# Conditioning projections of a two-layer diffusion trunk: from three ways of computing a block to one multiply-and-sum over transposed weights

## The chip, the cores and the metric

The kernel runs on one core of a Trainium2 chip. The metric is the device time of one execution in microseconds, as a median over runs. Engines are named as in the profile: PE (TensorE), DVE (VectorE), ACT (ScalarE), POOL (GpSimd) and SP (SyncE, which asks for most transfers). One core has 16 DMA engines.

## The reference, cut to what matters

Two layers over 512 latent tokens (128 to a tile) of width 1024, beside 256 context tokens that live through layer 0 only. Each layer begins with the six vectors of its adaptive norm:

```python
def ada_params(cond, w, b):          # cond (1, 1024), w (1024, 6144), b (6144)
    return jnp.split(jax.nn.silu(cond) @ w + b, 6, axis=-1)

for l in range(2):
    sh1, sc1, g1, sh2, sc2, g2 = ada_params(c, w_ada[l], b_ada[l])
    a = rms_norm(h, g_norm1[l]) * (1 + sc1) + sh1
    y = attention_mixer(a, ...) if l == 0 else conformer_conv(a, ...)
    h = h + g1 * y
    h = h + g2 * peer_ffn(rms_norm(h, g_norm2[l]) * (1 + sc2) + sh2, ...)
```

So per layer a matrix of 1024 x 6144 (24 MB) is multiplied by one row. `peer_ffn` scores 16 sets of 128 keys for each token, takes the best 16 of each, combines them, and mixes the values of 16 experts for each of 8 heads out of 16384 experts. The attention mixer has eight global heads with low-rank projections (`cq`, `ckv`) and eight neighbourhood heads (`qn`, `kn`, `vn`).

## The kernel before

One vector of 1024 is eight **blocks** of 128 columns; a layer has 48 blocks, numbered f = 0 to 47. Shifts and scales are needed as columns (`par`, 128 partitions x 48), the gates (blocks 16 to 23 and 40 to 47) as rows spread over all partitions, kept in DRAM (`g1d`, `g2d`) until they are used. A block's weights come as one tile `ada_w`, 128 x 8 x 128 floats, 512 KB in pieces of 512 bytes. Layer 0's blocks 0 to 15, which both the latent and the context tokens need first, are summed on PE in a prologue (lines 971 to 1005); this stays. The other 80 are spread over the kernel and computed in three ways:

- **On DVE, as eight small products** (lines 766 to 768): layer 0's blocks 16 to 23, at every second step of the input projections. A step is a quarter of one product (`quarter`, two of eight slices of the inner dimension, for 4 or 6 token tiles; products ckv, cq, kn, qn, vn of widths 288, 384, 512, 512, 512 with 6, 4, 6, 4, 6 token tiles, so 20 quarters). A sum of ones on PE (line 907) and an addition on DVE (908) make it a row in all partitions, which SP stores. The weights of a quarter are split into a high part (ACT) and a remainder (DVE, `w_lo`, line 1043), the latter just ahead of its use.
- **On POOL** (lines 779 to 782): layer 0's blocks 24 to 39, in attention, one at every fourth unit of the neighbourhood heads and at every second of the global heads (a head has four units). A transposition on PE (900) and a sum and an addition on DVE (902, 903) end each.
- **On PE, sixteen products of matrix by column or column by matrix** (819, 821): 14 blocks of layer 1 between the heads of the first PEER's query stage (line 282, one each, two in the first two), 4 more in its gate stage (line 533), and 8 of layer 1's in the second PEER's query stage.
- **In the first PEER's main loop**, as eight products on DVE, four per round, and a sum of ones on PE (866 to 887): 30 blocks. The tile for them has one buffer.

A PEER stage has these parts in order. The query stage: 16 halves of heads, each a product of 24 matmuls on PE (`s`, lines 145 to 147), a score product (`scp`, 260) and top-16 searches on DVE; then seven chunks of the expert product (`EARLY`). A gate stage in which DVE builds one-hot tiles (`eij`, `ahl`, lines 456 and 458) and PE multiplies them. The main loop of 128 rounds, of which the first 96 compute a chunk ahead (three matmuls per slice, `s1`), take its activation (line 313), prepare values and gates (`prep`, 582 to 600) and add up the output (605); POOL fetches rows of experts for the last token tile (616), and DVE multiplies and sums them (624, 628).

Each engine works in its program's order. SP's requests also wait in order: a load waits until its buffer is free, and every later request of SP behind it.

Of the kernel before, what the change touches and what calls it, by code (L numbers as in the profile page):

```python
# [1 line left out]

# [37 lines left out]
B0, B1, B2, B3, FRONT_TWICE = 8, 6, 20, 40, (0, 1)  # L40

# [3 lines left out]
HOW = "vga"  # L45
ADA_KV = (3,)
ADA_NOT = tuple(range(4, 20, 2))
# [102 lines left out]
def peer(k, h, xr, h_done, A, sh, g2d, wq, sk, uT, un, vn, out_open, out_cb, side=None, front=None, slow=None):  # L150
# [116 lines left out]
    front_step = front and front(qp, lambda: psf.tile([128, TT, 128], F32, name="gp", bufs=4))  # L267
# [48 lines left out]
    while front_step is not None and front_step():  # L316
        pass
# [164 lines left out]
    side_step = side and side(gp, lambda: psf.tile([128, TT, 128], F32, name="scp", bufs=2))  # L482

# [32 lines left out]
    for b in range(nb):  # L516
# [15 lines left out]
        if side_step is not None:  # L532
            side_step()
    while side_step is not None and side_step():
        pass
# [42 lines left out]
    def prep(c, cu=None):  # L578
# [6 lines left out]
        w = bs.tile([128, NTD], F32, name="w_f", bufs=2)  # L585
# [5 lines left out]
        nc.vector.tensor_tensor(w.rearrange("p (b t) -> p b t", t=SB), ring.pop(c).rearrange("p (b t) -> p b t", t=SB),  # L591
# [79 lines left out]
    beside = slow(bs) if slow is not None else None  # L671
    if beside is not None:
        next(beside)
# [4 lines left out]
    for m in range(NCHUNK):  # L678
# [8 lines left out]
        if c < NCHUNK:  # L687
            room = s1p[c][:, NTD:T]
            s1_gelu(c)
# [58 lines left out]
class Ada:  # L748
# [3 lines left out]
    def __init__(self, k, l, cond, w, bT, brow):  # L752
        self.k, self.l, self.cond, self.w, self.bT, self.brow = k, l, cond, w, bT, brow
        self.par = k.const.tile([128, 48], F32, name="ada_par%d" % l)

    def load(self, pool, f0, bufs):
        t = pool.tile([128, KD, 128], F32, name="ada_w", bufs=bufs)
        self.k.nc.sync.dma_start(t, self.w[:, f0:f0 + 128].rearrange("(kk p) f -> p kk f", p=128))
        return t

    def partial(self, how, t, acc):

        nc = self.k.nc
        c = self.cond
        if how == "v":
            nc.vector.tensor_scalar(acc, t[:, 0, :], c[:, 0:1], None, op0=OP.mult)
            for kk in range(1, KD):
                nc.vector.scalar_tensor_tensor(acc, t[:, kk, :], c[:, kk:kk + 1], acc, op0=OP.mult, op1=OP.add)
            return
        g = nc.gpsimd  # L770
        for kk in range(KD):
            if how == "a" or (how == "m" and kk % 2):
                nc.scalar.activation(t[:, kk, :], t[:, kk, :], AF.Copy, scale=c[:, kk:kk + 1])
        if how == "m":
            t2 = t.rearrange("p (k two) f -> p k two f", two=2)[:, :, 0, :]
            g.tensor_tensor(t2, t2, c.rearrange("p (k two) -> p k two", two=2)[:, :, 0:1].to_broadcast([128, 4, 128]),
                            op=OP.mult)
        if how == "g":
            g.tensor_tensor(t, t, c[:, :, None].to_broadcast([128, KD, 128]), op=OP.mult)
        g.tensor_tensor(t[:, 0:4, :], t[:, 0:4, :], t[:, 4:8, :], op=OP.add)  # L780
        g.tensor_tensor(t[:, 0:2, :], t[:, 0:2, :], t[:, 2:4, :], op=OP.add)
        g.tensor_tensor(acc, t[:, 0, :], t[:, 1, :], op=OP.add)

    def stepper(self, pool, psum, blocks, eng, g1_dst, g2_dst, lag=1, wbufs=2):

        nc = self.k.nc
        todo, loaded, accs, stores = list(blocks), [], [], []

        def reduce(f, acc):
            p = psum()  # L790
            if f // 8 in (2, 5):
                o = f % 8 * 128
                br = pool.tile([128, 128], F32, name="ada_br", bufs=lag)
                nc.sync.dma_start(br, row_bcast(self.brow[f * 128:(f + 1) * 128], 128))
                self.bcast(p[:, 0, :], acc[:, 0, :], br, br)
                stores.append(((g1_dst if f < 24 else g2_dst)[:, o:o + 128], br))
            else:
                self.columns(p, acc, f, 1)

        summed = []  # L800

        def on_pe():

            if stores:
                nc.sync.dma_start(*stores.pop(0))
            if summed:
                f, p, br = summed.pop(0)
                if br is None:
                    nc.vector.tensor_tensor(self.par[:, f:f + 1], p[:, 0, 0:1], self.bT[:, f:f + 1], op=OP.add)
                else:  # L810
                    nc.vector.tensor_tensor(br, p[:, 0, :], br, op=OP.add)
                    o = f % 8 * 128
                    stores.append(((g1_dst if f < 24 else g2_dst)[:, o:o + 128], br))
            if loaded:
                f, t, br = loaded.pop(0)
                p, c = psum(), self.cond
                for kk in range(KD):
                    if br is None:
                        nc.tensor.matmul(p[:, 0, 0:1], lhsT=t[:, kk, :], rhs=c[:, kk:kk + 1], start=(kk == 0), stop=(kk == KD - 1))
                    else:  # L820
                        nc.tensor.matmul(p[:, 0, :], lhsT=c[:, kk:kk + 1].to_broadcast([128, 128]), rhs=t[:, kk, :],
                                         start=(kk == 0), stop=(kk == KD - 1))
                summed.append((f, p, br))
            if todo:
                f, br = todo.pop(0), None
                if f // 8 in (2, 5):
                    br = pool.tile([128, 128], F32, name="ada_br", bufs=wbufs + 2)
                    nc.sync.dma_start(br, row_bcast(self.brow[f * 128:(f + 1) * 128], 128))
                loaded.append((f, self.load(pool, f * 128, wbufs), br))
            return bool(todo or loaded or stores or summed)  # L830
        if eng == "p":
            return on_pe

        def step():
            if stores:
                nc.sync.dma_start(*stores.pop(0))
            if len(accs) == lag or accs and not loaded:
                reduce(*accs.pop(0))
            if loaded:
                f, ts = loaded.pop(0)  # L840
                acc = pool.tile([128, 1, 128], F32, name="ada_acc", bufs=lag)
                self.partial(eng, ts, acc[:, 0, :])
                accs.append((f, acc))
            if todo:
                f = todo.pop(0)
                loaded.append((f, self.load(pool, f * 128, wbufs)))
            return bool(todo or loaded or accs or stores)
        return step

    def slow(self, pool, blocks, dst=None):  # L850


        nc, c = self.k.nc, self.cond
        blocks, after = list(blocks), []

        def load(f):
            br = None
            if f // 8 in (2, 5):
                br = pool.tile([128, 128], F32, name="ada_br", bufs=2)
                nc.sync.dma_start(br, row_bcast(self.brow[f * 128:(f + 1) * 128], 128))  # L860
            return self.load(pool, f * 128, 1), br

        def products(t, acc, kks):
            for kk in kks:
                if kk == 0:
                    nc.vector.tensor_scalar(acc, t[:, kk, :], c[:, kk:kk + 1], None, op0=OP.mult)
                else:
# [1173 lines left out]
```

## Time and profile before

| | us |
|---|---|
| median of three runs | 3344.88 |
| the three runs | 3340.55, 3344.88, 5339.81 |
| the profiled execution | 3343.83 |
| its span, first to last instruction | 3342.1 |
| PE busy | 3207.8 |
| DVE busy | 2576.0 |
| ACT busy | 1288.2 |
| POOL busy | 976.1 |

The profile is one execution. Busy times are sums over an engine's instructions; an engine that waits for a semaphore isn't busy. The mean granted clock of PE is 0.982 of its full speed. In the windows the stages are: 0 to 66 us prologue, 66 to 243 input and low-rank projections, 243 to 512 attention with its output product, 512 to 670 the first PEER's query stage, 670 to 868 its gates, 868 to 1805 its main loop and end, 1805 to 2065 the convolution, 2065 to 3342 the second PEER in the same order.

### The profile page before, as it was taken

How to read it: one execution, taken by the hardware profiler on the slowest of the kernel's cores; microseconds unless marked ns; L12 is line 12 of the kernel's file. 1: busy time of each engine (PE TensorE's matmuls, PEld its weight loads, DVE VectorE, ACT ScalarE, POOL GpSimd, SP SyncE). 2: the span in 40 equal slices, each digit the busy share in tenths (PEclk: the TensorE clock that was granted, in tenths of full speed). 3: DMA queues.
4: the chain of work that ended last, by engine and by line, in shares of the span. 5: the costliest groups of instructions: out<-in, count | busy, mean ns of one | idle time of the engine just before them, and what ended most of it. 6: DMA issues, size and time to landing. Idle time of an engine off the chain costs nothing.

```text
span 3342.1 us, 45728 instructions
## 1 busy us (share of the span) xinstructions
PE 3207.8 (96%) x16982; PEld 2783.6 (83%) x16982; DVE 2576.0 (77%) x4732; ACT 1288.2 (39%) x2065; POOL 976.1 (29%) x800
## 2 busy tenths in 40 slices
PE   8889999988999999999999998988999999999999
PEld 5775568978999999999987867888999999999987
DVE  3657736889688888888876976899777777777777
ACT  3435533345433333333335234235533333333333
POOL 1347412300033333443430001320033333344330
PEclk9989999999999999999999998999999999999999
DMA  6412124346799999899893113326789888989985
GB/s 199 130 46 79 57 82 152 114 164 252 269 337 328 324 342 333 318 339 336 307 320 119 51 45 112 117 86 247 266 285 314 313 310 315 313 309 314 314 311 180
DMA packets 373679, 764.34 MB, mean 229 GB/s; under 512 B 24144, under 2 KB 221008, under 8 KB 366160
## 3 DMA queue, kind: packets, MB, share of 16 engines
q1 hardware_dynamic: 292816, 442.62, 38.8%
q0 software_dynamic: 73728, 268.47, 22.9%
q10 hardware_dynamic: 6912, 50.33, 3.7%
q8 instruction: 133, 2.18, 0.3%
q14 instruction: 90, 0.74, 0.1%
HBM read 702.61 MB, written 58.72 MB: 228 GB/s over the span
## 4 chain that ended last, share of the span: by engine, by line
PE 83%; DVE 11%; issue 3%; DMA 1%; ACT 1%; SPq 1%; POOL 0%; ACTq 0%; POOLq 0%; DVEq 0%
PE acc L605 30%; PE s L145 11%; PE s L147 11%; PE s L146 11%; DVE eij L456 3%; PE y L1636 2%; PE cz L145 2%; PE cz L147 2%; PE cz L146 2%; DVE ahl L458 1%; PE z L147 1%; PE z L145 1%; PE z L146 1%; PE ot L1421 1%; DVE u_lo L176 1%
## 5 line engine op out<-in xcount | busy, mean ns | idle before, releaser
L146 PE MATMUL s<-hhi,u_lo 128*128 128x384 f32 (+1 forms) x2304 | 791.2, 343 | 14.4 <-DVE u_lo L176 14.2
L145 PE MATMUL s<-hhi,u_hi 128*128 128x384 f32 (+1 forms) x2304 | 798.6, 347 | 3.0 <-ACT u_hi L172 3.0
L147 PE MATMUL s<-hlo,u_hi 128*128 128x384 f32 (+1 forms) x2304 | 790.6, 343 | 0.0
L616 POOL DMA_INDIRECT row<-in_u_dram,eidx x256 | 313.2, 1224 | 954.2 <-DVE row L624 455.7
L616 POOL DMA_INDIRECT row<-in_v_dram,eidx x256 | 348.8, 1362 | 518.8 <-DVE gacc L628 448.4
L582 ACT ACTIVATE v_hi<-v_raw 128x1024 fp32r<-128x1024 f32 x192 | 203.8, 1062 | 679.0 <-PE acc L605 609.9
L146 PEld LDWEIGHTS s<-hhi,u_lo 128*128 128x128 f32 x2304 | 436.2, 189 | 33.2 <-DVE u_lo L176 17.4
L584 DVE TENSOR_TENSOR v_lo<-v_raw,v_hi 128x1024 fp32r<-128x1024 f32 x192 | 235.2, 1225 | 291.4 <-ACT v_hi L582 275.8
L145 PEld LDWEIGHTS s<-hhi,u_hi 128*128 128x128 f32 x2304 | 436.4, 189 | 18.8 <-ACT u_hi L172 3.7
L147 PEld LDWEIGHTS s<-hlo,u_hi 128*128 128x128 f32 x2304 | 435.6, 189 | 10.2
L605 PE MATMUL acc<-v_hi,w_hi 128*128 128x512 f32 x1344 | 417.4, 391 | 0.8 <-ACT w_hi L593 0.8
L605 PE MATMUL acc<-v_hi,w_lo 128*128 128x512 f32 x1344 | 416.2, 391 | 0.0
L605 PE MATMUL acc<-v_lo,w_hi 128*128 128x512 f32 x1344 | 415.9, 390 | 0.0
L176 DVE TENSOR_TENSOR u_lo<-u_raw,u_hi 128x1024 fp32r<-128x1024 f32 x242 | 295.1, 1219 | 48.1 <-ACT u_hi L172 48.0
L628 DVE SCALAR_TENSOR_TENSOR gacc<-row,gwgt,gacc 128x1024 f32<-128x1024 f32 x254 | 325.6, 1282 | 4.7
L172 ACT ACTIVATE u_hi<-u_raw 128x1024 fp32r<-128x1024 f32 x288 | 302.3, 1050 | 14.6 <-ACT stg L475 11.0
L624 DVE SCALAR_TENSOR_TENSOR row<-row,hg 128x1024 f32<-128x1024 f32 x256 | 300.6, 1219 | 0.0
L605 PEld LDWEIGHTS acc<-v_lo,w_hi 128*128 128x128 f32 x1344 | 252.3, 188 | 55.9
L605 PEld LDWEIGHTS acc<-v_hi,w_lo 128*128 128x128 f32 x1344 | 252.2, 188 | 54.6
L605 PEld LDWEIGHTS acc<-v_hi,w_hi 128*128 128x128 f32 x1344 | 249.5, 188 | 40.8 <-ACT w_hi L593 1.2
L593 ACT ACTIVATE w_hi<-w_f 128x384 fp32r<-128x384 f32 x256 | 134.7, 526 | 319.5 <-DVE w_f L591 315.8
L313 ACT ACTIVATE ring<-s 128x384 f32<-128x384 f32 x256 | 125.8, 491 | 318.8 <-PE s L147 318.8
(442 smaller groups left out, 4917.6 us busy)
## 6 DMA issues: line engine op xcount, KB each, us to landing
u_raw<-in_uT_dram SPq DMA_DIRECT2D x256, 512.0 KB
v_raw<-in_v_dram SPq DMA_DIRECT2D x192, 512.0 KB
Gd<-stg ACTq DMA_DIRECT2D x48, 1024.0 KB
g_in<-Gd SPq DMA_DIRECT2D x128, 384.0 KB
ada_w<-in_w_ada_dram SPq DMA_DIRECT2D x80, 512.0 KB
u_raw<-in_v_dram SPq DMA_DIRECT2D x64, 512.0 KB
u_raw<-in_wq_dram SPq DMA_DIRECT2D x32, 512.0 KB
ada_w<-in_w_ada_dram SPq DMA_DIRECT2D x8, 1024.0 KB
```

Source lines behind the costliest of these rows:

```text
L145: nc.tensor.matmul(out, lhsT=lh, rhs=rh, start=first, stop=False)
L146: nc.tensor.matmul(out, lhsT=ll, rhs=rh, start=False, stop=False)
L147: nc.tensor.matmul(out, lhsT=lh, rhs=rl, start=False, stop=last)
L172: nc.scalar.activation(uh, u, AF.Copy)
L176: lo_eng.tensor_tensor(ul, u, uh.bitcast(F32), op=OP.subtract)
L582: nc.scalar.activation(vh, v, AF.Copy)
L584: nc.vector.tensor_tensor(vl, v, vh.bitcast(F32), op=OP.subtract)
L593: nc.scalar.activation(wh, w, AF.Copy)
L605: nc.tensor.matmul(acc[tt][hf], lhsT=w[:, s], rhs=v[:, hf * 512:(hf + 1) * 512], start=f and n == 0, stop=l and n == 2)
L616: nc.gpsimd.indirect_dma_start(out=r, out_offset=None, in_=un if n < 128 else vn, in_offset=bass.IndirectOffsetOnAxis(ap=eidx[:, c:c + 1], ...
L624: nc.vector.scalar_tensor_tensor(r, r, 1.0, hg, op0=OP.mult, op1=OP.mult, accum_out=act[:, c:c + 1])
L628: nc.vector.scalar_tensor_tensor(gacc, r, wgt[:, c:c + 1], gacc, op0=OP.mult, op1=OP.add)
```

## The change

Every one of the 80 blocks is now computed in one way. The host gives the weights transposed (`wT_ada`, 6144 x 1024), so that a block's 128 outputs lie on partitions. A half block, 128 x 512 floats (256 KB in pieces of 2 KB), is multiplied on DVE by silu(c), which stands as a row in all partitions (`crow`), and summed along the row by the same instruction, into a column of `par` (first half) or of `half` (second half). After eight blocks two small additions join the halves and the bias. Gates are stored as 1024 floats, in pieces of 4 bytes, and read back spread over the partitions (`gate_row`). Each pool has two half buffers, and the load of the next half stands ahead of the multiplication in program order. A step of the generator `blocks` is one half.

Placement: layer 0's blocks 16 to 39 in the projections, three halves per quarter from the fourth quarter on, none left out; layer 0's 40 to 47 and layer 1's 0 to 7 in attention, two halves per step; layer 1's 8 to 39 in the first PEER's main loop, two halves in three rounds; layer 1's 40 to 47 in the second PEER's main loop, a half in four rounds. The query stages and the gate stage hold none. POOL and PE have no part in it. In the prologue the row of c is loaded to all partitions, and silu is taken on ACT and DVE ahead of the first modulation (`Am`); the bias column is copied. The prologue's weights become an array of their own (1024 x 2048). Besides, the product of gate and activation is written over the activation's buffer instead of into `w_f`, and the second PEER's modulation scale is computed before the convolution instead of behind it.

```diff
-B0, B1, B2, B3, FRONT_TWICE = 8, 6, 20, 40, (0, 1)
-HOW = "vga"
-ADA_NOT = tuple(range(4, 20, 2))
...
-def peer(k, h, xr, h_done, A, sh, g2d, wq, sk, uT, un, vn, out_open, out_cb, side=None, front=None, slow=None):
+def peer(k, h, xr, h_done, A, sh, g2d, wq, sk, uT, un, vn, out_open, out_cb, slow=None):
...
-        if front_step is not None:
-            front_step()
-            if hp in FRONT_TWICE:
-                front_step()
...
-        if side_step is not None:
-            side_step()
...
-        w = bs.tile([128, NTD], F32, name="w_f", bufs=2)
+        w = ring.pop(c)
...
-    beside = slow(bs) if slow is not None else None
-    if beside is not None:
-        next(beside)
+    beside = slow(bs)
...
-        if beside is not None and c < NCHUNK:
-            try:
-                beside.send(room)
-            except StopIteration:
-                beside = None
+        next(beside, None)
         if m == busy:
             nc.sync.dma_start(hres, hd)
-            nc.sync.dma_start(hg, g2d)
+            nc.sync.dma_start(hg, gate_row(g2d))
...
+        self.half = k.const.tile([128, 8], F32, name="ada_half%d" % l)
+        self.gate = {g: k.dram.tile([8, 128], F32, name="gate%d%d" % (l, g)) for g in (2, 5)}
+
+    def blocks(self, pool, blocks, pause=0):
+
+        nc, todo, loaded = self.k.nc, [(f, i) for f in blocks for i in range(2)], []
+
+        def load():
             if todo:
...
+                f, i = todo.pop(0)
+                t = pool.tile([128, D // 2], F32, name="ada_w", bufs=2)
+                nc.sync.dma_start(t, self.wT[f * 128:(f + 1) * 128, i * 512:(i + 1) * 512])
+                loaded.append((f, i, t))
+        load()
+        yield
+        while loaded:
+            load()
+            f, i, t = loaded.pop(0)
+            nc.vector.scalar_tensor_tensor(t, t, 1.0, self.k.crow[:, i * 512:(i + 1) * 512], op0=OP.mult, op1=OP.mult,
+                                           accum_out=self.half[:, f % 8:f % 8 + 1] if i else self.par[:, f:f + 1])
+            if f % 8 == 7 and i:
+                o = slice(f - 7, f + 1)
+                nc.vector.tensor_tensor(self.half, self.half, self.bT[:, o], op=OP.add)
+                nc.vector.tensor_tensor(self.par[:, o], self.par[:, o], self.half, op=OP.add)
+                if f // 8 in self.gate:
+                    nc.sync.dma_start(self.gate[f // 8].rearrange("f p -> p f"), self.par[:, o])
+            for _ in range(1 + pause):
+                yield
+
+
+def gate_row(g):
+    return g.rearrange("f p -> (f p)").partition_broadcast(128)
...
+    k.crow = k.const.tile([128, D], F32, name="crow")
+    cr = pp.tile([128, D], F32, name="cr")
+    nc.sync.dma_start(cr, row_bcast(a["crow"], D))
...
+    S.activation(k.crow, cr, AF.Sigmoid)
+    V.tensor_tensor(k.crow, cr, k.crow, op=OP.mult)
...
+    gate_blocks = ada.blocks(adp, range(16, 40))
+
+    def ada_step():
+        next(gate_blocks, True)
+        next(gate_blocks, True)
+        return next(gate_blocks, True)
...
-        if m not in ADA_NOT:
-            ada_step()
+        ada_step()
...
+    next_blocks = chain(ada.blocks(adp, range(40, 48)), ada1.blocks(adp, range(8)))
...
+        next(next_blocks, True)
+        return next(next_blocks, True)
...
+        def beside0(pool):
+            for n, _ in enumerate(ada1.blocks(pool, range(8, 40))):
+                yield
+                if n % 2:
+                    yield
+
+        def beside1(pool):
+            yield from ada1.blocks(pool, range(40, 48), 3)
...
+        A2 = modulation(k, k.const, g2T[1], ada1.par, 32, "A2_1")
         with k.pool("hA1") as hA:
             xr = conv(k, a, h, xr, nxt["xp"], hA, ada1)
-        A2 = modulation(k, k.const, g2T[1], ada1.par, 32, "A2_1")
```

## Rows read from the trace of the kernel before

**Rows 1.** The page: busy us per engine (share of span); shares of the chain.
```profile
PE 3207.8 (96%) x16982; PEld 2783.6 (83%) x16982; DVE 2576.0 (77%) x4732; ACT 1288.2 (39%) x2065; POOL 976.1 (29%) x800
...
PE 83%; DVE 11%; issue 3%; DMA 1%; ACT 1%; SPq 1%; POOL 0%; ACTq 0%; POOLq 0%; DVEq 0%
```
**Rows 2.** Windows: stretch, length; busy PE, PEld, DVE, ACT, POOL; clock, DMA share, GB/s.
```profile
66.00:145.00 79.00, 75.91 (x387) 65.88 (x385) 42.63 (x83) 37.60 (x79) 15.93 (x12) 1.00 0.47 146
145.00:210.00 65.00, 52.92 (x207) 42.52 (x208) 34.94 (x58) 14.39 (x27) 20.90 (x21) 0.87 0.16 48
...
243.00:460.00 217.00, 206.12 (x893) 119.77 (x892) 151.68 (x277) 113.57 (x287) 110.70 (x122) 0.96 0.19 57
...
630.00:670.00 40.00, 40.00 (x227) 37.89 (x226) 37.28 (x251) 15.52 (x21) 19.05 (x8) 1.00 0.31 106
...
868.00:1671.00 803.00, 802.24 (x4090) 731.30 (x4089) 685.98 (x1033) 291.32 (x387) 303.73 (x238) 1.00 0.92 327
```
**Rows 3.** Chain of waits, first PEER's query stage: start us, length us, what.
```profile
557.44 1.68 PE gp L819 x16
...
565.58 1.68 PE gp L819 x16
...
630.64 0.89 PE scp L260 x8
...
636.99 0.89 PE scp L260 x8
...
674.89 1.06 ACT u_hi L172
```
**Rows 4.** Chain of waits, start of the second PEER.
```profile
2060.86 2.24 DVE A L917
```
**Rows 5.** Timeline of ACT, line 313, chunks 31 and 127 of each PEER: start, length.
```profile
870.91 0.49 ACT L313 ACTIVATE ring<-s 128x384 f32<-128x384 f32 x1 [2.72 <-PE s L147]
...
1671.42 0.49 ACT L313 ACTIVATE ring<-s 128x384 f32<-128x384 f32 x1 [2.05 <-PE s L147]
...
2407.32 0.49 ACT L313 ACTIVATE ring<-s 128x384 f32<-128x384 f32 x1 [2.72 <-PE s L147]
...
3200.61 0.49 ACT L313 ACTIVATE ring<-s 128x384 f32<-128x384 f32 x1 [2.05 <-PE s L147]
```
**Rows 6.** Waits of PE, 66 to 215 us: for whom, us, times, longest.
```profile
PE z L147 <- DVE w_lo L1043: 10.8, 2, 6.0
PE tp L907 <- DVE ada_acc L768: 3.9, 1, 3.9
```
**Rows 7.** Chain of waits, projections.
```profile
161.50 3.30 DMA g1d<-ada_br
```
**Rows 8.** Chain of waits, global heads of attention.
```profile
367.40 5.29 PE ot L1421 x12
...
376.20 1.54 DVE ada_par L903
...
383.06 5.29 PE ot L1421 x12
...
401.66 5.29 PE ot L1421 x12
416.06 5.29 PE ot L1421 x12
```
**Rows 9.** Groups by line: count, shortest, median, longest ns of one instruction.
```profile
L768 DVE SCALAR_TENSOR_TENSOR ada_acc<-ada_w,cond,ada_acc x56: 350/352/2585, 80.1 to 204.4; 128x128 f32<-128x128 f32 x56
...
L624 DVE SCALAR_TENSOR_TENSOR row<-row,hg x256: 1215/1220/1224, 909.7 to 2854.2; 128x1024 f32<-128x1024 f32 x128
L624 DVE DVE_READ_ACCUMULATOR row<-row,hg x256: 80/82/88, 910.8 to 2855.3; 128x1 f32 x128
...
L1757 DVE SCALAR_TENSOR_TENSOR cv<-pad,vec,cv x124: 717/747/752, 1844.0 to 1982.2; 128x512 f32<-128x512 f32 x124
```
**Rows 10.** Groups by line: loads of ACT's function table at line 955.
```profile
L955 ACT ACT_TABLE_LOAD  x1: 1283/1283/1283, 0.7 to 0.7; - x1
```

More of the change, by code (lines that the diff above doesn't have):

```diff
@@ L1 @@
 from contextlib import ExitStack
+from itertools import chain
 import numpy as np
@@ L314, in s1_gelu @@
         ring[c] = r
-    while front_step is not None and front_step():
-        pass
     for c in range(EARLY):
@@ L687, in peer @@
         if c < NCHUNK:
-            room = s1p[c][:, NTD:T]
             s1_gelu(c)
@@ L748, with __init__ @@
 class Ada:
-    def __init__(self, k, l, cond, w, bT, brow):
-        self.k, self.l, self.cond, self.w, self.bT, self.brow = k, l, cond, w, bT, brow
+    def __init__(self, k, l, wT):
+        self.k, self.l, self.wT = k, l, wT
         self.par = k.const.tile([128, 48], F32, name="ada_par%d" % l)
[L756 to L823, printed above, removed]
-            if todo:
[L825 to L867, printed above, removed]
-                    nc.vector.scalar_tensor_tensor(acc, t[:, kk, :], c[:, kk:kk + 1], acc, op0=OP.mult, op1=OP.add)
-        t, br = load(blocks[0])
-        yield
-        for n, f in enumerate(blocks):
-            acc = pool.tile([128, 128], F32, name="ada_acc", bufs=2)
-            if after:
-                after.pop(0)()
-            products(t, acc, range(4))
-            yield
-            if after:
-                after.pop(0)()
-            products(t, acc, range(4, KD))
-            now = br
-            p = yield
-            if now is None:
-                nc.tensor.matmul(p[:, 0:1], lhsT=acc, rhs=self.k.ones[:, 0:1], start=True, stop=True)
-                after.append(lambda f=f, p=p: nc.vector.tensor_tensor(self.par[:, f:f + 1], p[:, 0:1], self.bT[:, f:f + 1], op=OP.add))
-            else:
-                nc.tensor.matmul(p, lhsT=self.k.ones, rhs=acc, start=True, stop=True)
-                after.append(lambda p=p, br=now: nc.vector.tensor_tensor(br, p, br, op=OP.add))
-                after.append(lambda f=f, br=now: nc.sync.dma_start(dst[:, f % 8 * 128:(f % 8 + 1) * 128], br))
-            if n + 1 < len(blocks):
-                t, br = load(blocks[n + 1])
-            yield
-        while after:
-            after.pop(0)()
-            yield
@@ L896, in columns @@
-    def columns(self, p, acc, f, n):
-        nc = self.k.nc
-        for i in range(n):
-            nc.tensor.transpose(p[:, i, :], acc[:, i, :], self.k.ident)
-        o = self.par[:, f:f + n]
-        nc.vector.tensor_reduce(o, p[:, 0:n, :], axis=AX.X, op=OP.add)
-        nc.vector.tensor_tensor(o, o, self.bT[:, f:f + n], op=OP.add)
-    def bcast(self, p, acc, dst, brow):
-        nc = self.k.nc
-        nc.tensor.matmul(p, lhsT=self.k.ones, rhs=acc, start=True, stop=True)
-        nc.vector.tensor_tensor(dst, p, brow, op=OP.add)
+        self.half = k.const.tile([128, 8], F32, name="ada_half%d" % l)
@@ L977, in attention @@
             nc.sync.dma_start(vt, a["vec0"])
-    ada.bT = vecs["bT0"]
+    ada.bT = k.const.tile([128, 48], F32, name="bT0")
+    V.tensor_copy(ada.bT, vecs["bT0"])
+    k.crow = k.const.tile([128, D], F32, name="crow")
+    cr = pp.tile([128, D], F32, name="cr")
+    nc.sync.dma_start(cr, row_bcast(a["crow"], D))
     ada1.bT = k.const.tile([128, 48], F32, name="bT1")
     nc.sync.dma_start(ada1.bT, a["bT1"])
-    k.g1d = [k.dram.tile([128, D], F32, name="g1d%d" % l) for l in range(2)]
-    k.g2d = [k.dram.tile([128, D], F32, name="g2d%d" % l) for l in range(2)]
     ss = pp.tile([128, 6], F32, name="ss")
@@ L1117, in attention @@
     r1 = lst.enter_context(k.pool("a_r1"))
-    ada_step = ada.stepper(adp, lambda: psz.tile([128, 4, 128], F32, name="tp", bufs=2), range(16, 16 + B0), HOW[0], k.g1d[0], None)
+    gate_blocks = ada.blocks(adp, range(16, 40))
[3 more added lines that the diff above has]
+        return next(gate_blocks, True)
     qn = r1.tile([128, 4, 8, 64], F32, name="qn")
@@ L1321, in attention @@
     q_half(1)
-    while ada_step():
+    while ada_step() is None:
         pass
@@ L1508, in attention @@
     g1b = hA.tile([128, D], F32, name="g1b")
-    nc.sync.dma_start(g1b, k.g1d[0])
-    ada_ps = lambda: psh.tile([128, 4, 128], F32, name="pt", bufs=3)
-    steps = [ada.stepper(adp, ada_ps, range(16 + B0, 40), HOW[1], None, None)]
+    nc.sync.dma_start(g1b, gate_row(ada.gate[2]))
+    next_blocks = chain(ada.blocks(adp, range(40, 48)), ada1.blocks(adp, range(8)))
     def ada_step():
-        if steps and not steps[0]():
-            steps.pop(0)
-        return steps
+        next(next_blocks, True)
+        return next(next_blocks, True)
     units = [(kind, hd, m) for kind in "nm" for hd in range(8) for m in range(4)]
@@ L1560, in attention @@
         due.pop()()
-    while ada_step():
+    while ada_step() is None:
         pass
@@ L1706, in conv @@
     ns.close()
-    nc.sync.dma_start(g1b, k.g1d[1])
+    nc.sync.dma_start(g1b, gate_row(ada.gate[2]))
     nc.sync.dma_start(b2b, row_bcast(a["b_pw2"], D))
@@ L1908, in trunk @@
         hs = ExitStack()
-        ada0 = Ada(k, 0, None, a["w_ada0"], None, a["b_ada0"])
-        ada1 = Ada(k, 1, None, a["w_ada1"], None, a["b_ada1"])
+        ada0, ada1 = (Ada(k, l, a["wT_ada%d" % l]) for l in range(2))
         R = dict(side="right")
@@ L1932, in done1 @@
                 nxt["nr"].add(tt, y)
[L1934 to L1939 removed]
+        def beside0(pool):
[5 more added lines that the diff above has]
+            yield from ada1.blocks(pool, range(40, 48), 3)
         A2 = modulation(k, k.const, g2T[0], ada0.par, 32, "A2_0")
[L1942 to L1943 removed]
+        peer(k, h, xr, hs.close, A2, ada0.par[:, 24:32], ada0.gate[5], a["wq0"], a["sk0"], a["uT0"], a["u0"], a["v0"],
+             open1, done1, beside0)
         h, xr = nxt["h"], nxt["nr"].finish()
+        A2 = modulation(k, k.const, g2T[1], ada1.par, 32, "A2_1")
         with k.pool("hA1") as hA:
             xr = conv(k, a, h, xr, nxt["xp"], hA, ada1)
[L1947 removed]
         def store(tt, y, hf):
@@ L1951, in store @@
             nc.sync.dma_start(out[tt * 128:(tt + 1) * 128, d], y[:, d])
-        peer(k, h, xr, hn.close, A2, ada1.par[:, 24:32], k.g2d[1], a["wq1"], a["sk1"], a["uT1"], a["u1"], a["v1"],
-             None, store, None, front(range(B3, 48)))
+        peer(k, h, xr, hn.close, A2, ada1.par[:, 24:32], ada1.gate[5], a["wq1"], a["sk1"], a["uT1"], a["u1"], a["v1"],
+             None, store, beside1)
 def layout(inp):
```

19 lines of the change are left out of this document (4 added, 15 removed).

## The prediction

> **What bounds the kernel now.** I read the page first: TensorE (PE) is busy for 96% of the span and carries 83% of the chain of waits, VectorE (DVE) 11% of it [rows 1]. So an instruction taken off PE is worth its own length wherever PE never waits, and less where it does. That has to be asked stage by stage, and the table of windows answers it [rows 2]. In 868 to 1671 us (main loop of the first PEER) PE is busy for 802.2 of 803 us, in 630 to 670 (query stage of the first PEER) for 40.0 of 40. There PE is the limit and nothing else. In the projections (66 to 210) it is busy for 128.8 of 144 us, and its granted clock is 0.87 in the second part, a mean of stretches at the full level (2.4 GHz) and the half (1.2). In attention (243 to 460) it is busy for 206.1 of 217 at a clock of 0.96. In these two stages DVE or a load ends some of the waits. The work that the change touches lies in all of these stages, so the forecast is a sum over five places.
>
> **Query stages.** The 14 blocks of the first PEER's query stage and the 8 of the second's lose their sixteen PE products each. Priced from the chain: a head with a block takes 565.58 - 557.44 = 8.14 us, one without takes 636.99 - 630.64 = 6.35 [rows 3]. That is 1.79 us per block, on an engine that is never idle there: 14 x 1.78 = 24.9 us and 8 x 1.78 = 14.2 us (I price the second PEER's blocks by the first's, the products being of the same kind and number). What could be late next is DVE with its top-16 searches: in the stretch without blocks it is busy for 37.3 of 40 us while PE still stands at 40.0 [rows 2]. So it fits, with 7% to spare, and it has the seven expert chunks behind the query in which to catch up. What hides it is thin, and that is a rival below.
>
> The first PEER's gate stage held four more blocks on PE beside its gate products. By the same price that is 7.1 us at most and nothing at least. I take 6, near the upper end, because PE ends most of that stage too and only a few of its waits are for others.
>
> **Main loops.** In the first PEER's loop the change removes 30 small sums on PE, 240 products of 128x128 on DVE and a load that the loop starts with. The second PEER's loop is the same loop without any such work: from the last activation of a chunk before the loop to the last in it (96 chunks) it takes 3200.61 - 2407.32 = 793.3 us, the first PEER's 1671.42 - 870.91 = 800.5 [rows 5]. Gain 7.2 us, if the new work there costs nothing. The new work is 64 half blocks on DVE in about 96 rounds, and 16 in the second PEER's 96 rounds. A multiply-and-sum over 128x1024 takes 1.22 us plus 0.08 for the read of the accumulator [rows 9]. Half the columns make 0.61 us. Bounds: 0.57, if the fixed part is nothing, to 0.83, from a two-input operation of 128x512 at 0.747 plus that read. So 0.4 to 0.55 us per round of 8.3 us, where 240 x 0.35 / 96 = 0.9 leave. What covers it is a DVE that is 85% busy with the old work (686.0 of 803 [rows 2]). If that cover failed, the sum would lose these 7 us and no more. The bytes loaded are the same in halves; DMA is already at 0.92 of its time there, and PE has not noticed.
>
> Modulation of the second PEER's input is computed before the convolution now and not behind it. That takes DVE's 2.24 us at 2060.86 off the chain [rows 4]; I take 2.
>
> Sum of the PEER parts: 24.9 + 14.2 + 6 + 7.2 + 2 = 54.3 us. It is the solid part.
>
> **Projections.** Removed: 8 blocks of small products on DVE, at 8 x 8 x 0.352 = 23 us undisturbed [rows 9] and their additions, about 24, and 8 pairs of PE sums. With them go PE's waits of 10.8 us for a weight remainder that stood behind these products on DVE, and 3.9 us for the products themselves [rows 6]. A clock of 0.87 over 65 us costs up to 8 us, which I put down to those waits. So 23 us could come back.
> Added: 48 half blocks, three per step, in 16 steps. 48 x 0.61 = 29 us of DVE. And a wait: there are two buffers, so the third half of a step is loaded into the buffer that the first half of the same step gives free. DVE then stands until that load lands. The nearest row is a store of 64 KB, 3.30 us on the chain [rows 7]; less the 0.61 of the second half, 2.7 us per step. The bounds are 0 and, if the load queues behind weight loads on SP, about 5. Per step DVE is held for 3 x 0.61 + 2.7 = 4.5 us, and behind the waiting instruction stand the weight remainders that PE needs. Old DVE work is (42.6 + 34.9 - 24) / 20 = 2.7 us per quarter product [rows 2], so a step asks 7.2 us of DVE.
> PE's quarters, by columns (128.8 us over 4 x (1536 + 1728 + 2048 + 2 x 3072) = 45,800 token-tile columns, 2.8 ns each), take 4.3 us for cq, 5.8 for qn, 8.6 for kn and vn. So the four cq quarters fall short by 2.9 us each and the four qn ones by 1.4: 17 us, of which I leave 2 to work done ahead: 15, plus 4 for the clock (half of the old 8, since the new waits are shorter ones). Net 23 - 19 = 4 us gained. Bounds: 18 gained if the load lands in time, 8 lost if the wait is nearer to 5.
>
> The stores of the gates go out in 4-byte pieces and are read back stages later, so they hide behind everything in between; if they were slow, SP's next half load would start later, which the bounds above contain. The POOL work in this stage stays.
>
> **Attention.** Removed: 16 blocks on POOL with a transposition on PE and two DVE operations each. Heads with this work take 383.06 - 367.40 = 15.7 us and once 401.66 - 383.06 = 18.6, without it 416.06 - 401.66 = 14.4; the second of the DVE operations stands on the chain with 1.54 us [rows 8]. Three heads at 1.3 and one at 4.2 make 8 us for the eight blocks of the global half; for the eight of the neighbourhood half, which has no undisturbed head to compare with and where POOL works beside it too, I take 12 as an estimate. So 20 us hang on 16 blocks. Added: 32 half blocks, two per step, whose loads were asked a step before: 1.22 us of DVE per block, in place of the 1.54 and about 0.2 of the other operation. So I give back 20 x 1.22 / 1.74 = 14. Net 6 us gained, between 14 (DVE, busy for 151.7 of 217 us [rows 2], hides most of it) and 3 lost (all of it on the path, and a wait for a load besides).
>
> **Prologue.** Behind the first modulation sums and ahead of the first activations of x there come a sigmoid over 128x1024 on ACT, 1.06 us by the row of the same shape [rows 3], perhaps with a table load of 1.28 [rows 10], and a DVE product of 1.2. ACT can do its part early if its load is there: 1 to 5 us lost, I take 3. The weights of the first sums become a shorter array read in the same pieces: nothing.
>
> **Sum.** 54.3 + 4 + 6 - 3 = 61.3 us. The profiled execution took 3343.8 us (span 3342.1), about 1 us under the median of 3344.9, so 3343.8 - 61.3 = 3282.5 us. 2% of the median, about what a measurement of this kernel can tell from no change, is 66.9 us, hence the line stands at 3278.0. My sum comes out just inside it.
>
> **A rule that speaks against it.** The longest of the old small products took 2.585 us where the median took 0.352 [rows 9]: something held DVE. POOL is busy for 15.9 + 20.9 = 36.8 us of the projections [rows 2], and the new instruction, like the old one, reads two tiles from SBUF. The Trainium skill, "SBUF — State Buffer", section "Who interferes with whom", says that a VectorE instruction with two SBUF inputs contends with a GpSimd instruction that reads SBUF; the long case agrees with it, though the row does not say who held it. By this rule the gain of the projections would go, since 48 instructions can be held where 64 shorter ones were. Priced from the rows: all 36.8 us of POOL on DVE's path, in steps that are level already, make 3282.5 + 36.8 = 3319 us.
>
> **Rivals.**
> (a) The projections hold: loads land in time and attention keeps its 14: 54.3 + 18 + 14 - 2 = 84 us, 3260 us. For it: the load is small and asked for as soon as its buffer is free. Against it: the third half cannot be asked for earlier than in its own step. Chance 0.30.
> (b) DVE becomes the bound of the query stages. If top-16 work needs 6% more than PE's 6.35 us, 32 heads lose 12 us: 3294 us. For it the 93% of DVE; against it PE's full busy time beside that. Chance 0.10.
> (c) DVE's new instructions are held while POOL works, as the longest old ones were: 3319 us as above, chance 0.06. Against it is the median of 0.352 in the same stretch: most were not held.
> (d) Slower than before: waits for the loads in the projections. With a round trip r a step asks 1.83 + r - 0.61 + 2.7 us of DVE; 16 steps reach the present 144 us plus the 57 us gained elsewhere at r = 8.6 us. At 10 us they take 223 us, 79 more than now: 3343.8 + 79 - 57 = 3366 us. For it: the loads stand in SP's queue among weight loads. Against: the nearest round trip is 3.3 us. Chance 0.04.
> My forecast has 0.50.
>
> **The numbers.** About a quarter of the forecast's 0.50 lies beyond the 2% line, which is only 4.5 us off, and so does (a): 0.12 + 0.30 = 0.42 faster. Of (d), half is slower by over 2%, which takes round trips above 12 us: 0.02. The rest, 0.56, is within. The range begins at (a) with attention's new products wholly hidden (6 more), the prologue free (2) and the side blocks at their 7.1: 3250. It ends where projections and attention stand at their lower bounds (12 and 9 less than taken), the prologue at 5 and the main loop gives nothing: 61.3 - 12 - 9 - 2 - 7 = 31 us gained, 3312. Above it are left (c) and (d), below it little.
>
> **What would show it.** Query stages: PE gapless and heads of 6.35 us throughout; a wait of PE for a score's copy there would speak for (b). First main loop: 793 us over its 96 chunks. Projections: in each step DVE stands about 2.7 us for a half-block load; if it does not, (a). Attention: heads near 15 us with no POOL beside them. The forecast is wrong if PE's new waits in the projections are not between 10 and 25 us.

## The result, and the profile after

The median fell from 3345.4 to 3323.4 us; the ratio is 0.9935, with a 95% interval of 0.9918 to 0.9952. That is a gain of 22 us, clear of the measurement's own scatter but a third of the 61 forecast, and outside the range (3250 to 3312). The profiled execution took 3326.2 us, its span is 3324.3.

The page of the changed kernel, beside [rows 1]: PE has lost 38 us of work, but its share of the chain fell by five points, and transfers, 1% before, now end 5% of it.

```profile
PE 3169.6 (95%) x16474; PEld 2736.3 (82%) x16474; DVE 2547.0 (77%) x4674; ACT 1288.6 (39%) x2066; POOL 942.5 (28%) x736
...
PE 78%; DVE 12%; DMA 5%; issue 3%; ACT 2%; SPq 1%; POOL 0%; ACTq 0%; DVEq 0%; POOLq 0%
```

To see where the gain went I set one landmark per stage against the same landmark of before (start times in us, from timelines and groups; the last column is how much longer or shorter the stage before it became):

| landmark | before | after | stage |
|---|---|---|---|
| first product of the neighbourhood heads (`ot`) | 253.7 | 261.8 | +8.1 |
| first product of the global heads (`ot`) | 351.7 | 377.7 | +17.9 |
| attention's output product (`y`) | 458.6 | 480.4 | -4.2 |
| first table load for the experts' activations | 646.8 | 645.2 | -23.4 |
| last activation in the first main loop | 1671.4 | 1660.3 | -9.5 |
| convolution's first sum (`cv`) | 1843.1 | 1835.7 | +3.7 |
| the same table load, second PEER | 2188.7 | 2165.0 | -16.3 |
| last activation in the second main loop | 3200.6 | 3182.5 | +5.6 |
| end of the span | 3342.1 | 3324.3 | +0.3 |

The query stages and the gate stage gave what they should. Projections, attention and the main loops lost it again. Of the first 8.1 us only 2.4 lie in prologue and projections: attention's first transposition (`pt<-ident,qn`) starts at 231.5 us before and at 233.9 after, and the rest passes between it and the first product of the heads. The chain names a first cause: close behind each of the four gate stores stands one long transfer (chain of waits of the changed kernel; start, length, what).

```profile
112.16 13.15 DMA ada_w<-in_wT_ada_dram
...
352.80 12.08 DMA ada_w<-in_wT_ada_dram
...
1276.48 18.21 DMA v_raw<-in_v_dram
...
2899.27 15.69 DMA v_raw<-in_v_dram
```

A half block elsewhere in the projections lands in 2.5 us, on the same view: these waits are not the price of the load itself.

```profile
79.40 2.53 DMA ada_w<-in_wT_ada_dram
...
85.28 2.52 DMA ada_w<-in_wT_ada_dram
```

The main loops show what the two late ones cost. From the activation of chunk 31 to that of chunk 127 [rows 5], the first loop takes 1660.29 - 863.33 = 797.0 us (800.5 before, 793.3 forecast), the second 3182.46 - 2383.17 = 799.3 (793.3 before, and forecast).

```profile
863.33 0.49 ACT L305 ACTIVATE ring<-s 128x384 f32<-128x384 f32 x1 [2.72 <-PE s L144]
...
1660.29 0.49 ACT L305 ACTIVATE ring<-s 128x384 f32<-128x384 f32 x1 [1.55 <-PE s L144]
...
2383.17 0.49 ACT L305 ACTIVATE ring<-s 128x384 f32<-128x384 f32 x1 [2.72 <-PE s L144]
...
3182.46 0.49 ACT L305 ACTIVATE ring<-s 128x384 f32<-128x384 f32 x1 [2.17 <-PE s L144]
```

### The profile page after: what moved, and what is told of

Its sections match the earlier page's. It is cut to its first block, busy times and chain, and to the rows that moved or that the text cites. A ratio compares the mean times of both kernels' runs of the same rounds, so it can differ in the third digit from the quotient of the medians.

```text
span 3324.3 us, 44464 instructions
## 1 busy us (share of the span) xinstructions
PE 3169.6 (95%) x16474; PEld 2736.3 (82%) x16474; DVE 2547.0 (77%) x4674; ACT 1288.6 (39%) x2066; POOL 942.5 (28%) x736
## 4 chain that ended last, share of the span: by engine, by line
PE 78%; DVE 12%; DMA 5%; issue 3%; ACT 2%; SPq 1%; POOL 0%; ACTq 0%; DVEq 0%; POOLq 0%
PE acc L589 29%; PE s L144 10%; PE s L143 10%; PE s L142 10%; DVE eij L446 3%; PE y L1496 2%; PE cz L142 2%; PE cz L144 2%; PE cz L143 2%; DMA ada_w<-in_wT_ada_dram 2%; DVE ahl L448 1%; DVE u_lo L173 1%; PE ot L1283 1%; PE z L144 1%; DMA u_raw<-in_v_dram 1%
## 5 line engine op out<-in xcount | busy, mean ns | idle before, releaser
L600 POOL DMA_INDIRECT row<-in_u_dram,eidx x256 | 346.6, 1354 | 919.4 <-PE acc L589 440.9
L589 PEld LDWEIGHTS acc<-v_lo,w_hi 128*128 128x128 f32 x1344 | 252.7, 188 | 56.0
L577 ACT ACTIVATE w_hi<-ring 128x384 fp32r<-128x384 f32 x256 | 134.6, 526 | 321.9 <-DVE ring L575 319.2
```

The costliest lines, as they stand in the source:

```text
L577: nc.scalar.activation(wh, w, AF.Copy)
L589: nc.tensor.matmul(acc[tt][hf], lhsT=w[:, s], rhs=v[:, hf * 512:(hf + 1) * 512], start=f and n == 0, stop=l and n == 2)
L600: nc.gpsimd.indirect_dma_start(out=r, out_offset=None, in_=un if n < 128 else vn, in_offset=bass.IndirectOffsetOnAxis(ap=eidx[:, c:c + 1], ...
```

## The experiments

Theory G: a gate store in 4-byte pieces holds the transfers behind it. Rival W: the missing time is the wait for the third half of each step in the projections, and the products themselves. Spans are those of the profiled executions; the changed kernel's is 3324.3. Its four executions took 3318.4 to 3326.2 us, and the profiled one is the longest of them. act_queue, twice, aq_global and aq_split were executed once, the other kernels four times, so a difference of a few us against one of those four proves little by itself.

**rows32: the stores in pieces of 32 bytes.**

```diff
-        self.gate = {g: k.dram.tile([8, 128], ...
+        self.gate = {g: k.dram.tile([128, 8], ...
...
-                    nc.sync.dma_start(self.gate[f // 8].rearrange("f p -> p f"), self.par[:, o])
+                    nc.sync.dma_start(self.gate[f // 8], self.par[:, o])
```

> The changed kernel with one thing different: each of the four gate stores writes its 1024 floats in the order in which they lie in SBUF, 128 pieces of 32 bytes in place of 1024 pieces of 4; the readers take the row through a reordered view. Theory G (the stores in 4-byte pieces hold every later transfer of the same queue; the chain of the changed kernel shows loads of 13.2, 12.1, 18.2 and 15.7 us just behind the four stores): these four waits go, the first product of the global heads falls from 377.7 to about 352 us, the second main loop from 799 to about 793.5, and the time from 3323 to 3285 (3275 to 3297). Rival W (the wait for the third half of each step, and the multiplications themselves, cost the missing 40 us): the time stays above 3312.

3311.7 us (ratio to before 0.9909, 0.9892 to 0.9926), span 3309.6: 15 us less (12 by the medians), not 38. That is the edge of rival W's range. By landmarks the second loop is back at 793.8 us, the first global product at 361.6 (from 377.7). The reordered view costs DVE some 2 us in the convolution and 2 at the end. G is right as a mechanism and too small as a sum: something else keeps some 20 us.

**act_queue: the stores as they were, asked for by ACT.**

```diff
-                    nc.sync.dma_start(self.gate[f // 8].rearrange("f p -> p f"), self.par[:, o])
+                    nc.scalar.dma_start(self.gate[f // 8].rearrange("f p -> p f"), self.par[:, o])
```

> The changed kernel with the four gate stores, still in pieces of 4 bytes, asked for by ACT instead of SP. If the loads wait because they stand behind the store in SP's own order of transfers (theory G, in the form of a queue), they no longer do: about 3285 us (3275 to 3300), nearly as with larger pieces. If the small pieces occupy the DMA engines themselves, whoever asks: 3310 to 3325. Rival W: 3323.

3306.0 us, span 3304.1: between the two ranges, and both readings have a part in it. Both loops take what was forecast, 793.7 and 794.1 us, and 20 us of the span come back, so the place behind the store in SP's queue did cost time. But small pieces from ACT's queue slow SP's loads too. In the projections the second half block behind the first store (asked 1.6 us after it) took 13.15 us in the changed kernel; here, asked 0.6 us after it, it takes 11.0, and in rows32 4.2. Two behind the second store take 7.8 us, in rows32 2.7 and 3.0 (groups of these loads; act_queue, then rows32, then the same for the second store).

```profile
L743 SPq DMA_DIRECT2D ada_w<-in_wT_ada_dram x1: 328/328/328, 111.6 to 111.6; - x1
...
DMA to landing us min/median/max: 11.0/11.0/11.0
...
L743 SPq DMA_DIRECT2D ada_w<-in_wT_ada_dram x1: 376/376/376, 110.0 to 110.0; - x1
...
DMA to landing us min/median/max: 4.2/4.2/4.2
...
L743 SPq DMA_DIRECT2D ada_w<-in_wT_ada_dram x2: 328/328/328, 352.4 to 353.0; - x2
...
DMA to landing us min/median/max: 7.8/7.8/7.8
...
L743 SPq DMA_DIRECT2D ada_w<-in_wT_ada_dram x2: 328/328/328, 348.5 to 349.1; - x2
...
DMA to landing us min/median/max: 2.7/2.8/3.0
```

How much of the 20 us is the order in SP's queue alone is not separated. The store itself is as slow from ACT's queue, here from issue to landing (group of line 757):

```profile
L757 ACTq DMA_DIRECT2D gate<-ada_par x4: 366/396/422, 111.0 to 2883.7; - x4
...
DMA to landing us min/median/max: 10.0/11.8/24.4
```

and in pieces of 32 bytes (the same group in rows32):

```profile
L757 SPq DMA_DIRECT2D gate<-ada_par x4: 326/326/331, 108.6 to 2887.0; - x4
...
DMA to landing us min/median/max: 1.4/2.4/4.6
```

4 KB take 11.8 us in 1024 pieces and 2.4 in 128.

**twice: each store made a second time.**

```diff
                     nc.sync.dma_start(self.gate[f // 8].rearrange("f p -> p f"), self.par[:, o])
+                    nc.sync.dma_start(self.gate2[f // 8].rearrange("f p -> p f"), self.par[:, o])
```

> The changed kernel with each of the four gate stores made twice, the second into a tensor that nobody reads. Theory G: each store adds its wait once more, 35 to 55 us in all: 3358 to 3378. Rival W: within 5 us of 3323.

3337.7 us, span 3335.9: 11.6 more, above the rival's 5 but far below 35. The second store, asked 0.4 us after the first, lands after the same time (group of the second store's line; the first has 10.5/12.1/13.0):

```profile
DMA to landing us min/median/max: 11.3/12.3/15.4
```

So two stores run side by side, and most of the wait is not paid twice. I had priced the store as work; for the most part it is a delay. The 11.6 us are not explained; 7.4 of them lie in the first main loop (804.3 us against 797.0 from chunk 31 to chunk 127). What makes a store so long is not shown.

**rows32_two: two halves per step in the projections, on top of rows32.**

```diff
-    gate_blocks = ada.blocks(adp, range(16, 40))
+    gate_blocks = chain(ada.blocks(adp, range(16, 48)), ada1.blocks(adp, range(8)))
...
-        next(gate_blocks, True)
         next(gate_blocks, True)
         return next(gate_blocks, True)
...
-    while ada_step() is None:
-        pass
...
-    next_blocks = chain(ada.blocks(adp, range(40, 48)), ada1.blocks(adp, range(8)))
+    next_blocks = gate_blocks
```

> The kernel with 32-byte gate stores, and two halves per step in the projections instead of three, the halves that are left over going into attention's steps (two per step, 22 of its 24 steps in place of 17). No load then has to land within its own step. If the in-step wait is a cost of its own (rival W, or a second term beside G), the projections give back 8 to 15 us and attention loses about 5: 5 to 10 us under the kernel with 32-byte stores alone. If the wait is hidden, the two differ by under 3 us, or this one is slower by the products added in attention.

3297.5 us, 14 less than rows32 (expected 5 to 10). The first neighbourhood product comes at 245.1 us instead of 253.0; DVE's waits for half blocks fall from 30.3 to 8.8 us, PE's for weight remainders from 11.4 to 4.4 (waits, 66 to 215 us). The in-step wait is a cost of its own: 8 us at this landmark, where the prediction had put 14 between the wait and loads that land in time (4 and 18 gained). The projections also hold fewer products now, so the 8 us are not the wait's alone; another 5 come from the global heads, where a loss was expected, and why is open. The wait is no part of the miss: with it, rows32 reaches this landmark at 253.0, where 252.7 were forecast (253.7 - 4 + 3). That close a match is luck. In rows32 attention's first transposition starts at 225.2 us, 6.3 earlier than before, where 1 was forecast, and from there to the landmark it takes 27.8 us, before 22.2.

**Where the rest was.** In act_queue the eight neighbourhood heads still take 95.5 us from first to last product, 84.0 before. The windows of the two, before and act_queue, columns as in [rows 2]:

```profile
253.70:337.70 84.00, 80.32 (x373) 49.34 (x372) 66.46 (x137) 45.02 (x136) 60.36 (x79) 0.96 0.24 72
```
```profile
256.90:352.40 95.50, 86.37 (x366) 51.37 (x366) 60.20 (x150) 44.12 (x134) 22.41 (x43) 0.89 0.18 60
```

DVE and POOL do less than before, and still PE stands idle for 9 us and runs at a lower clock. One head of act_queue shows why (timeline; start, length, engine, line, operation, idle before):

```profile
276.86 0.70 DVE L1317 TENSOR_SCALAR Pr<-Pr,z 128x448 f32<-128x448 f32 x1
...
277.48 0.94 DVE L750 SCALAR_TENSOR_TENSOR ada_w<-ada_w,crow 128x512 f32<-128x512 f32 x1
...
278.35 0.93 DVE L750 SCALAR_TENSOR_TENSOR ada_w<-ada_w,crow 128x512 f32<-128x512 f32 x1
...
279.22 0.42 DVE L1305 TENSOR_TENSOR sc<-sc,nbias 128x256 f32<-128x256 f32 x1
...
281.58 0.33 PE L1330 MATMUL pt<-ident,Pr 128*128 128x128 f32 x1 [1.69 <-DVE kT L1231]
```

Two products in a row hold the next unit's softmax for 1.74 us (277.48 to 279.22). PE waits for the copy `kT`, which stands behind that softmax in DVE's order, and is idle for 1.69. The granted clock is 1.00 from 272.1 to 281.5 us and 0.50 from 282.3 to 288.9, behind this gap; over the head (269.7 to 285.0 us) it is 0.83.

**aq_global and aq_split: attention's halves placed otherwise,** both on top of act_queue, aq_global first.

```diff
-        if i % 4 == 0 if kind == "n" else i % 2 == 0:
-            ada_step()
+        if kind == "m":
+            next(next_blocks, True)
```
```diff
-        if i % 4 == 0 if kind == "n" else i % 2 == 0:
-            ada_step()
+        if i % 2 == 0 if kind == "n" else True:
+            next(next_blocks, True)
```

> The kernel with the gate stores on ACT's queue, and one more thing different: attention's 32 half blocks go into the units of the global heads alone, one per unit, and none into the neighbourhood heads. Theory N (in the neighbourhood heads two products in a row, 0.9 us each beside POOL, stand on DVE between a unit's softmax and the next; PE is left idle for 1.5 us per head and then runs at the half clock: 0.85 to 0.9 granted): without them these heads take 10.2 to 11.5 us again at a clock of 1.00, the stretch from the first neighbourhood product to the first global one falls from 109.7 to about 96 us, the global heads grow by 1 to 3 us in all, and the time from 3306 to about 3294 (3289 to 3299). Rival P (the heads were faster before because PE's transpositions of the old blocks or POOL's work kept the engines in step, and the new products have no part in it): the heads stay at 12.5 to 15 us and the time within 4 us of 3306.

> The kernel with the gate stores on ACT's queue; attention's half blocks are the same in each kind of head, but one at a time: at every second unit of the neighbourhood heads and at every unit of the global ones. Theory N: a single product of 0.7 to 0.9 us fits into the slack of a unit, so most of the loss goes: 96 to 103 us for the neighbourhood heads, 3294 to 3301. If any product there costs its own length and the clock, the stretch stays at 106 to 110 us.

3289.9 and 3287.6 us, the second 6 us under its range. The neighbourhood heads, aq_split first, then aq_global:

```profile
252.20:336.10 83.90, 79.06 (x365) 48.34 (x364) 61.21 (x153) 44.58 (x136) 21.08 (x43) 0.96 0.22 72
```
```profile
258.90:336.80 77.90, 77.15 (x366) 47.66 (x365) 52.69 (x122) 44.61 (x134) 19.29 (x43) 0.98 0.13 40
```

The same 366 PE instructions that are busy for 86.4 us beside pairs are busy for 77.2 us without products: 9 us of the loss are the clock and 8 are idle time. One product at a time, though as many of them, gives 12 of these 18 us back. Rival P, that PE's old transpositions or POOL had kept the engines in step, falls.

Single products give 6 us more ahead of these heads, and there the pairs are not the whole cause. From attention's first transposition to the first product of the heads it takes 22.2 us before, 27.9 in act_queue, 21.9 in aq_split, but 26.5 in aq_global too, which has no product there. In act_queue and aq_global a normalisation on DVE (`Pr`) takes 4.18 and 4.19 us while POOL runs five operations on two tiles each (TENSOR_TENSOR); DVE then works without a pause up to the copy `kT`, and PE waits for that (timelines; act_queue, aq_global, aq_split).

```profile
245.31 4.18 DVE L1317 TENSOR_SCALAR Pr<-Pr,z 128x448 f32<-128x448 f32 x1
253.00 0.69 PE L1330 MATMUL pt<-ident,Pr 128*128 128x128 f32 x2 [3.83 <-DVE kT L1231]
...
248.69 4.19 DVE L1317 TENSOR_SCALAR Pr<-Pr,z 128x448 f32<-128x448 f32 x1
255.16 0.58 PE L1330 MATMUL pt<-ident,Pr 128*128 128x128 f32 x2 [2.41 <-DVE kT L1231]
...
244.54 0.68 DVE L1317 TENSOR_SCALAR Pr<-Pr,z 128x448 f32<-128x448 f32 x1
```

So this part hangs on which DVE instruction meets POOL's work. In aq_split none does so for long, and that may be luck: no run places it on purpose. The kernel before has two such long ones, of 3.6 us, without a wait of PE over 0.3 us behind them.

**split_alone: the changed kernel with single products in attention and nothing else.**

> The changed kernel itself, gate stores as they are, with one thing different: attention's half blocks come one at a time (at every second unit of the neighbourhood heads, at every unit of the global ones) instead of two in a row at every fourth and second. If the cost of the pairs in the neighbourhood heads is independent of the gate stores: 14 to 20 us under the changed kernel, 3303 to 3310. If the gain of the split kernels came from the store's queue and the pairs together: less than 8 us, 3315 or more.

3309.0 us (0.9887, 0.9871 to 0.9904): 14 us under the changed kernel, with the gate stores untouched, where beside the moved stores it was 18 (3306.0 to 3287.6). So the second cause does not need the first.

**aq_two_global and aq_two_split: all of it together.**

> All three at once: gate stores on ACT's queue, two half blocks per step in the projections, and the remaining 44 halves in the global heads (three per two units), none in the neighbourhood heads. Theory N and the in-step wait together: about 13 us from the neighbourhood heads and 12 from the projections, less 5 for 12 more products in the global heads: 3286 (3279 to 3293). If the terms only move the bound elsewhere: 3297 or more.

> Gate stores on ACT's queue, two half blocks per step in the projections, the other 44 halves in attention one at a time. Against the kernel that puts these 44 into the global heads alone (3281.5): the neighbourhood heads cost about 7 us more, as in the pair of kernels with three per step (97.7 against 90.7 us), the global heads about 7 less. 3276 to 3286. If it is over 3286, the two ways of placing them aren't equal.

3281.5 us (0.9814, 0.9798 to 0.983) and 3277.4 us (0.9802, 0.9786 to 0.9819). The second beats the kernel before by 67 us and the changed one by 46.

## Why the prediction was wrong

Point by point, by its own steps:

- **Prologue: right.** The projections' first products, of latent and context tokens, start at 47.4 and 50.7 us before and at 49.0 and 53.7 after: 1.6 and 3.0 us lost, 3 forecast.
- **Query stages: right.** Heads of 6.34 us, without a gap (chain of the changed kernel, as in [rows 3]). The stage is 23.4 us shorter from `y` to the table load, where 24.9 were forecast; the second PEER's 16.3, where 14.2 and the 2 of the modulation were. DVE held up: rival (b) falls.

```profile
622.65 0.89 PE scp L257 x8
628.99 0.89 PE scp L257 x8
635.34 0.89 PE scp L257 x8
```

- **Gate stage: right.** From the first `eij` to the activation of chunk 31: 167.7 us before, 161.7 after; 6 forecast.
- **Main loops: right for the products, wrong for what came with them.** Without the queued stores both take 794 us, as forecast. A product takes 0.685 us there, between the bounds, and hides.
- **Projections: the wait right, the gain too small.** A half block lands in 2.5 us on the chain; DVE's waits for half blocks are 37.4 us, 2.3 per step (2.7 forecast), PE's for remainders 13.4 us (10 to 25). Rival (a) falls: the wait is there, and rows32_two shows that it has a price. Without slow stores (rows32) the stage ends 6.3 us earlier than before, prologue included, where 1 was forecast.

```profile
DVE ada_w L750 <- DMA ada_w<-in_wT_ada_dram: 37.4, 24, 6.8
...
PE z L144 <- DVE w_lo L901: 13.4, 7, 5.2
```

- **"The stores of the gates [...] so they hide behind everything in between": the step that failed first.** I looked at who reads the row, which is stages later. Of what stands behind a store I named only the next half load in the projections, not the loads behind the other three, in attention and the main loops. And my "bounds above" end at a wait of about 5 us, with no row for a transfer of 1024 pieces; the nearest I took was 3.30 us [rows 7]. The store takes 11.8 us, and a half block behind the first one 13.15. It cost about 20 us: 3324.3 - 3304.1 with act_queue; rows32 gives back 15 and pays 4 for its reordered view.
- **Attention's "net 6 us gained": the step that failed second.** From the first product of the heads to `y` it takes 204.9 us before; 198.9 were forecast, and act_queue takes 215.1. I charged DVE's products by their length against the length of what they replace. For the neighbourhood heads I estimated a gain of 12 us that was not there to be had: without any block in them (aq_global) they take 77.9 us where they took 84.0, and five of seven head periods before were gapless, 53.12 us busy of 53.40 at a clock of 1.00 (window of before):

```profile
253.70:307.10 53.40, 53.12 (x256) 33.05 (x255) 44.68 (x95) 30.30 (x94) 48.08 (x66) 1.00 0.30 93
```

  PE is full there and each unit passes through DVE, so two products at once opened gaps, and the clock about doubled their price (8 us idle, 9 by the clock). Placing them singly gives 18.6 us back (3304.1 - 3285.5). By landmarks 12 of these lie in the neighbourhood heads, 6 in the wait ahead of their first product, of which POOL has a part, and 3 in the global heads; the other stages together are 2.6 us longer. aq_split's 199.9 us from the first product to `y` are near the forecast, but the gain is not where I put it: it comes from the global heads (106.9 to 102.2), and the neighbourhood heads give nothing.

Both together take the changed kernel's span to 3285.5 us, and its time to 3287.6, 5 us from the 3282.5 forecast. The remaining 5 us are not settled; by the landmarks of aq_split no stage is more than 1.4 us off its forecast, the end of the first PEER being the furthest.

Rival (c) shows itself in part. In the changed kernel's projections 12 of the 48 products take 0.91 to 2.88 us, each of them beside a TENSOR_TENSOR operation of POOL, and the other 36 take 0.68 to 0.69: 9.4 us more in all on DVE, and not the 37 of the rival.

```profile
L750 DVE SCALAR_TENSOR_TENSOR ada_w<-ada_w,crow x48: 680/692/2882, 71.9 to 207.0; 128x512 f32<-128x512 f32 x48
```

In the neighbourhood heads of act_queue the eight products beside such operations take 0.905 to 0.944 us, the others 0.68 to 0.69. Beside POOL's fetches of rows, in the main loops, they take 0.685. How much of this reached PE is not shown. The Trainium skill's rule, "SBUF — State Buffer", section "Who interferes with whom", that DVE with two inputs in SBUF contends with POOL where POOL reads SBUF, agrees with these rows: the product has two such inputs.

## What to carry to other kernels

A transfer's price is also what it does to those behind it in its queue: ask for each new store how many pieces it has and which load stands next. Where PE is gapless, look at the chain that each unit takes through the other engines before adding work there, and try it in single pieces rather than in pairs; in these heads a gap was paid twice, once as idle time and once in the clock. Look also at what POOL does beside a DVE instruction that such a chain waits for. A landmark per stage, set beside the sum's terms, finds the wrong term in one view, if the landmark stands at the stage's border: the first product of the heads hid 6 us of attention in the projections' term.

## What the runs showed of the hardware

- 4 KB stored from SBUF to DRAM in 4-byte pieces took 10 to 24 us to land, in 32-byte pieces 1.4 to 4.6. During it the 16 DMA engines moved 15 and 12 GB/s and were busy for 0.14 and 0.19 of their time (windows of the changed kernel behind the first store; the last three columns are clock, DMA share and GB/s). A second such store beside it took no longer (run twice). Asked for by another queue, such a store still slowed loads: 11.0 us in place of 4.2 for a half block (act_queue, rows32).

```profile
113.50:117.00 3.50, 3.50 (x19) 2.89 (x18) 0.69 (x1) 2.27 (x3) 0.00 (x0) 1.00 0.14 15
117.00:120.00 3.00, 3.00 (x15) 2.49 (x14) 0.00 (x0) 0.00 (x0) 0.00 (x0) 1.00 0.19 12
```

- PE's mean granted clock was 0.98 in heads with 0.8 us of idle time in 78 us (aq_global) and 0.89 in the same heads with 9.1 us in 96 (act_queue), with the same instructions. Behind one gap of 1.69 us it was 0.50 for 6.6 us.
- Beside TENSOR_TENSOR operations of POOL, DVE's multiply-and-sum over 128x512 took 0.905 to 2.88 us in place of 0.68 to 0.69, and a normalisation over 128x448 4.19 us in place of 0.45 to 0.81.
